# Zero-padded operands in index scores and linear attention, and a new product order in a recurrence

## The chip, the cores and the metric

One core of a Trainium2 chip runs the whole kernel. The metric is device time in microseconds, the median of several runs. The kernel before takes 2926.25 us (three runs, 2922.95 to 2929.03).

## What is computed

Two layers of a streaming encoder, 256 positions, width 2048, in float32. Each layer normalises its input, projects it with one wide matrix to the columns of four mixers, and merges the mixers' outputs behind sigmoid gates. The change touches three of the mixers:

```
# B, sparse attention: scores of all keys for each query, 8 index heads of width 64
rel   = relu(einsum('bqhd,bsd->bqhs', iq, ik))
score = einsum('bqh,bqhs->bqs', iw, rel)            # top 64 of them are kept

# A, gated linear attention, chunks of 64 positions, 4 heads (dk 128, dv 256)
k_dec = k_c * exp(total - cum)
state = state * exp(total) + einsum('bchk,bchv->bhkv', k_dec, v_c)
out   = einsum('bchk,bhkv->bchv', q_c, state)

# C, RWKV-7: a delta-rule state of 64 x 64 per head, 16 heads, here in chunks of 64
state = state*w + (state @ -kk) (kk*a)^T + v k^T ;   y = state @ r
```

D is a gated MLP that the change leaves alone. Index keys `ik` are shared by the eight heads.

## The kernel before

The 256 positions lie as two row tiles of 128 partitions. All large products go through one weight stream: SyncE fetches a block of weights of 128 x 4 x 512 (`raw`, three buffers), ScalarE rounds each 128 x 512 tile to float32r (`wh`, line 154 by `act`), VectorE takes the rest (`wl`, line 157 by `tt`), three buffers each, and TensorE adds three products for each operand pair: high x high, high x low, low x high (`mm` where positions are the output's rows, `mc` and `mb` where channels are too). All matrix products are recorded at line 169, transposes at 173, whatever calls them, so rows are told apart by tile names.

The order on each engine is set by a scheduler, which places instructions by priority and by its own simulated times; each engine then runs its list in order. Stream products thus stand between the small products of a mixer and fill TensorE while those wait for ScalarE or VectorE.

The three places that the change touches:

* **Index scores** (`b_index`). For each row tile `t` and index head one product `psc` of the head's 64 channels (`iqT`, on partitions 0 to 63 or 64 to 127 by the head's parity) with the keys `ikT`, which lie twice, once on either half of the partitions (made in `small`). ScalarE takes the ReLU into `rl`, VectorE adds it with weight `iw` into `bias`, and then finds the top 64 with eight rounds of MAX and MATCH_REPLACE in the same tile. On the same VectorE list stand the 62 steps of a triangular solve (`slv`, `slvt`) of the recurrence.
* **Recurrence** (`c_chain`). For each chunk `q` and each half `g` of the heads: `pW` (for q > 0 a 128 x 128 product of `AR` and state `sbd`, and for each of two heads a product of `G` with `VU` on 64 output rows), copied to `wbd`; `pU` from `wbd`, copied to `VU`; `pS` for the next state; `pY` for the output. All four live in a PSUM ring of two buffers (`pc`).
* **Linear attention** (`a_head`). For each head and row tile two products `pkv` of 64 positions each (keys with decay times values, one chunk each), VectorE chains them into states `aS`, and two products `pao` of 64 query positions each with the chunk's state fill the halves of one output tile.

A ring `zz` of two tiles of 128 x 1024, filled with zeros by GpSimd (`zero_padded`, line 492), holds operands whose other half stays zero: `arbd`, `wbd`, `sbd`.

Of the kernel before, what the change touches and what calls it, by code (L numbers as in the profile page):

```python
# [16 lines left out]
I32 = mybir.dt.int32  # L17
AF = mybir.ActivationFunctionType
OP = mybir.AluOpType
# [109 lines left out]
class Trunk:  # L129
# [188 lines left out]
    def rope_tables(self):  # L318
        nc = self.nc
        inv = self.inv  # L320
        pi = self.one([128, 2], "posi", I32)
        nc.scalar.dma_start(pi, self.i["positions"].rearrange("b (t p) -> p (b t)", p=128))
        pf = self.one([128, 2], "posf")
        nc.vector.tensor_copy(pf, pi)
        tb = lambda name: self.one([128, 2, 16], name)
        ang, n1, n2, tmp = tb("ang"), tb("n1"), tb("n2"), tb("rtmp")
        for t in range(2):
            self.ts(ang[:, t, :], inv, pf[:, t:t + 1], OP.mult)
        magic = 12582912.0
        i2 = float(np.float32(1.0 / (2.0 * np.pi)))  # L330

        def rnd(o, a, f):
            self.ts(o, a, f, OP.mult, magic, OP.add)
            self.ts(o, o, -magic, OP.add)


        rnd(n1, ang, i2 / 4096.0)
        self.stt(tmp, n1, -4096.0 * 2.0 * np.pi, ang, OP.mult, OP.add)
        rnd(n2, tmp, i2)
        for c in TWO_PI:  # L340
            self.stt(ang, n1, -4096.0 * c, ang, OP.mult, OP.add)
            self.stt(ang, n2, -c, ang, OP.mult, OP.add)
        rnd(n2, ang, i2)
        for c in TWO_PI:
            self.stt(ang, n2, -c, ang, OP.mult, OP.add)
        lim = 3.1415925
        self.ts(ang, ang, lim, OP.min, -lim, OP.max)
        self.sin, self.cos = tb("sin"), tb("cos")
        self.act(self.sin, ang, AF.Sin)
        self.ts(tmp, ang, -1.0, OP.mult)  # L350
        self.tt(tmp, tmp, ang, OP.max)
        self.ts(tmp, tmp, -1.0, OP.mult, float(np.float32(np.pi / 2)), OP.add)
        self.act(self.cos, tmp, AF.Sin)
        self.dump("cos", self.cos)
        self.dump("sin", self.sin)
# [86 lines left out]
    def small(self):  # L442
        nc, l = self.nc, self.l
        pa = self.product(self.xT, KT, 280, range(9), range(9))
        s = self.t("ev", [128, 2, 280], "small")
        for t in range(2):
            self.act(s[:, t, :], pa[t])
        self.w2 = self.t("s8", [97, 2, 1024], "w2")
        for a, b in ((0, 96), (96, 97)):
            nc.scalar.dma_start(self.w2[a:b], self.i["w2"][l, a:b])  # L450

        ps = self.pm([128, 2, 256], "trS")
        for j in range(2):
            for t in range(2):
                self.tr(ps[0:96, j, t * 128:(t + 1) * 128], s[:, t, j * 96:(j + 1) * 96])
        c = self.t("t2", [96, 2, 257], "lrc")
        nc.gpsimd.memset(c[:, :, 0:1], 0.0)
        self.act(c[:, :, 1:257], ps[0:96])
        d = self.t("t2", [96, 2, 256], "lrd")
        self.tt(d, c[:, :, 0:256], c[:, :, 1:257], OP.subtract)  # L460
        wT, aT = self.one([97, 256], "wT"), self.one([97, 256], "aT")
        nc.gpsimd.memset(wT, 1.0)
        nc.gpsimd.memset(aT, 1.0)
        self.stt(wT[0:96], d[:, 0, :], self.pcol[0:96, 48:49], c[:, 0, 1:257], OP.mult, OP.add)
        self.act(wT[0:96], wT[0:96], AF.Tanh)
        self.stt(aT[0:96], d[:, 1, :], self.pcol[0:96, 49:50], c[:, 1, 1:257], OP.mult, OP.add)
        self.wT, self.aT = wT, aT

        pg = self.pm([128, 256], "pg")
        for t in range(2):  # L470
            self.tr(pg[0:16, t * 128:(t + 1) * 128], s[:, t, 192:208])
        self.gT = self.one([17, 256], "gT")
        nc.gpsimd.memset(self.gT, 1.0)
        self.act(self.gT[0:16], pg[0:16])

        ik = s[:, :, 208:272].rearrange("p t (h d) -> p t h d", h=1)
        self.rope(ik, 8, 1, 2)
        ikd = self.t("s1", [128, 2, 2, 64], "ikd")
        nc.vector.tensor_copy(ikd, s[:, :, 208:272].unsqueeze(2).to_broadcast([128, 2, 2, 64]))
        pk = self.pm([128, 256], "pk")  # L480
        for t in range(2):
            self.tr(pk[:, t * 128:(t + 1) * 128], ikd[:, t].rearrange("p a d -> p (a d)"))
        self.ikT = self.one([128, 256], "ikT")
        self.act(self.ikT, pk)
        self.iw = self.one([128, 2, 8], "iw")
        self.ts(self.iw, s[:, :, 272:280], 512.0 ** -0.5, OP.mult)

# [176 lines left out]
    def c_chain(self, ys):  # L664

        nc = self.nc
        H = [slice(0, 64), slice(64, 128)]
# [3 lines left out]
        wbd, sbd = self.zero_padded("wbd"), self.zero_padded("sbd")  # L671
        for q in range(4):
            t, par = q // 2, q % 2
# [2 lines left out]
            G = self.t("s8", [128, 8, 2, 128], "Gq")  # L676
            nc.scalar.dma_start(G, self.Gd[:, qi])

            for g in range(2):
                pw = self.pc([128, 4, 128], "pW")  # L680
                for p in range(4):
                    if q:
                        self.mm(pw[:, p, :], self.AR[g][:, p, q].rearrange("p a t -> p (a t)"),
                                sbd[:, g][:, p].rearrange("p h v -> p (h v)"), p == 0, False, skip_group_check=True)
                    for h in range(2):
                        self.mm(pw[0:64, p, H[h]], G[:, 4 * g + p, 0, H[h]], self.VU[g][:, p, q, H[h]],
                                q == 0 and p == 0 and h == 0, True, skip_group_check=True)
                for h in range(2):
                    nc.vector.tensor_copy(wbd[:, g][H[h], :, h, :], pw[0:64, :, H[h]])
                if q:  # L690
                    self.act(Ys[g][O, t], pw[64:128])
# [7 lines left out]
            if q < 3:  # L699
                for g in range(2):  # L700
# [4 lines left out]
                    for h in range(2):  # L705
                        o = sbd[:, g][H[h], :, h, :]
# [56 lines left out]
    def b_index(self):  # L763
        nc = self.nc
# [5 lines left out]
        iqT = self.t("ev", [128, 4, 256], "iqT")  # L770
        for j in range(0, 4, 2):
            ps = self.pm([128, 2, 256], "piq")
# [5 lines left out]
        sc = self.bias  # L778
        for t in range(2):
            nk = 128 * (t + 1)  # L780
            for h in range(8):
                s = slice((h % 2) * 64, (h % 2) * 64 + 64)
                ps = self.pm([128, nk], "psc")
                self.mm(ps, iqT[s, h // 2, t * 128:(t + 1) * 128], self.ikT[s, 0:nk])
                rl = self.t("s1", [128, nk], "rl")
                self.act(rl, ps, AF.Relu)
                w = self.iw[:, t, h:h + 1]
                if h == 0:
                    self.ts(sc[:, t, 0:nk], rl, w, OP.mult)
                else:  # L790
                    self.stt(sc[:, t, 0:nk], rl, w, sc[:, t, 0:nk], OP.mult, OP.add)
            nc.vector.memset(sc[0:64, t, nk - 64:nk], NEG)
            if t == 1:
                self.dump("score", sc[:, 1, :])
            for _ in range(8):
                m8 = self.one([128, 8], "m8", bufs=2)
                nc.vector.max(m8, sc[:, t, 0:nk])
                nc.vector.match_replace(sc[:, t, 0:nk], m8, sc[:, t, 0:nk], HIT)
            self.ts(sc[:, t, 0:nk], sc[:, t, 0:nk], THR, OP.is_ge, BIG, OP.mult)
# [58 lines left out]
    def a_decay(self):  # L858
        nc = self.nc
# [15 lines left out]
        for t in range(2):  # L875
# [3 lines left out]
                self.mm(pt[:, h, 2 * t:2 * t + 2], lg[:, t, h * 128:(h + 1) * 128], self.ind)  # L879
            self.act(ex[:, t, :], pz, AF.Exp, scale=1.0 / 16)  # L880
        self.aex = ex
        self.atot = self.one([128, 4, 4], "atot")
        self.act(self.atot, pt, AF.Exp, scale=1.0 / 16)
        self.hg = self.t("bs", [128, 256], "hg")
# [2 lines left out]
    def a_head(self, h, g, ys):  # L887
        nc = self.nc
        pa = self.product(self.xT, KT, 512)
        m = self.t("ev", [128, 2, 512], "qkv")  # L890
        for t in range(2):
            self.act(m[:, t, :], pa[t])
        self.tt(m[:, :, 128:256], m[:, :, 128:256], self.aex[:, :, h * 128:(h + 1) * 128], OP.mult)
        ps = self.pm([128, 256], "paq")
        for t in range(2):
            self.tr(ps[:, t * 128:(t + 1) * 128], m[:, t, 0:128])
        qT = self.t("s1", [128, 256], "aqT")
        self.act(qT, ps, scale=128.0 ** -0.5)
        y = self.t("t2", [128, 2, 256], "ay")
        ss = self.one([128, 2], "ass", bufs=2)  # L900
        S = None
        for t in range(2):
            H = [slice(0, 64), slice(64, 128)]
            pk = [self.pc([128, 256], "pkv") for _ in range(2)]
            for par in range(2):
                self.mm(pk[par], m[H[par], t, 128:256], m[H[par], t, 256:512])
            Sq = []
            for par in range(2):
                q = 2 * t + par
# [6 lines left out]
                Sq.append(Sn)  # L916
            po = self.pm([128, 256], "pao")
            for par in range(2):
                q = 2 * t + par
                self.mm(po[H[par]], qT[:, q * 64:(q + 1) * 64], Sq[par])  # L920
            self.act(y[:, t, :], po, AF.Square, accum_out=ss[:, t:t + 1])
            self.rsqrt(ss[:, t:t + 1], ss[:, t:t + 1], 1.0 / 256, EPS)
            self.stt(y[:, t, :], po, ss[:, t:t + 1], self.hg, OP.mult, OP.mult)
# [149 lines left out]
```

## Time and profile before

| what | value |
|---|---|
| median of three runs | 2926.25 us |
| profiled execution | 2923.81 us, of it span 2922.0 us |
| mean granted TensorE clock | 0.997 |
| TensorE busy | 2878.9 us, 99% |
| VectorE busy | 1860.6 us, 64% |
| ScalarE busy | 1470.6 us, 50% |
| GpSimd busy | 196.6 us, 7% |
| DMA | 183 GB/s, 48.1% of the engines' time on the weight queue |

Busy time of TensorE counts pipelined products whose ends are modelled, so what a product costs is read from the starts of the products around it. A product with plain f32 operands shows as two records. `128*64` in a row means 128 rows and 64 columns of the array, `64*128` the reverse.

### The profile page before, as it was taken

Reading aid. Unit: us, or ns where it says so; the run is one execution under the profiler, and the core shown is the slowest. Engines: PE = TensorE matmul, PEld = TensorE weight load, DVE = VectorE, ACT = ScalarE, POOL = GpSimd, SP = SyncE. Lnnn points to the kernel's source line nnn. Section 1 sums busy time; section 2 is a strip of 40 time slices with the busy share of each in tenths; the row PEclk is TensorE's granted clock in tenths of the full one; section 3 lists DMA queues with packets and bytes.
Section 4 is the critical chain, followed back from the end, with each engine's and each line's share of the span. In section 5 each row is a group of like instructions: output and inputs, shape, how many; then the busy total and the mean of one; then the engine's idle time right before and its main releaser. Section 6 shows DMA issues by size and latency. Waiting matters only on the chain.

```text
span 2922.0 us, 44230 instructions
## 1 busy us (share of the span) xinstructions
PE 2878.9 (99%) x16880; PEld 2465.0 (84%) x16880; DVE 1860.6 (64%) x3347; ACT 1470.6 (50%) x2632; POOL 196.6 (7%) x291
## 2 busy tenths in 40 slices
PE   7999999999999999999989999999999999999998
PEld 6998888887778898888789988888877788988886
DVE  6787857655555655556568878575555556565565
ACT  6554544545444545445565555345554444454454
POOL 1222001000000000000022220110000000000000
PEclk9999999999999999999999999999999999999999
DMA  5555545555445565555555565355554555555554
GB/s 184 186 192 184 181 149 176 181 187 185 163 166 193 188 213 191 187 190 186 181 178 188 188 206 167 136 185 186 188 180 161 176 189 202 195 192 190 190 185 158
DMA packets 100796, 533.51 MB, mean 183 GB/s; under 512 B 30852, under 2 KB 31108, under 8 KB 40742
## 3 DMA queue, kind: packets, MB, share of 16 engines
q1 hardware_dynamic: 68256, 486.96, 48.1%
q10 hardware_dynamic: 26568, 24.85, 2.8%
q0 software_dynamic: 5760, 18.88, 2.0%
q8 instruction: 132, 2.16, 0.3%
q14 instruction: 80, 0.66, 0.1%
HBM read 512.83 MB, written 17.83 MB: 182 GB/s over the span
## 4 chain that ended last, share of the span: by engine, by line
PE 79%; issue 16%; DVE 2%; ACT 1%; DMA 1%; ACTq 0%; POOL 0%; DVEq 0%; POOLq 0%
PE mm L169 48%; PE mc L169 15%; PE mb L169 6%; PE pW L169 1%; DVE wl L157 1%; ACT wh L154 1%; PE pG L169 1%; PE pao L169 1%; PE pY L169 1%; PE pU L169 1%; PE pkv L169 1%; PE trT L173 0%; PE psc L169 0%; PE plg L169 0%; PE po L169 0%
## 5 line engine op out<-in xcount | busy, mean ns | idle before, releaser
L157 DVE TENSOR_TENSOR wl<-raw,wh 128x512 fp32r<-128x512 f32 (+1 forms) x1822 | 1255.0, 693 | 885.0 <-ACT wh L154 879.5
L154 ACT ACTIVATE wh<-raw 128x512 fp32r<-128x512 f32 (+1 forms) x1822 | 1145.8, 630 | 1264.8 <-DVE wl L157 619.4
L169 PE MATMUL mm<-wh,xT 128*128 128x512 f32 (+1 forms) x4216 | 1332.0, 393 | 2.6 <-ACT wh L154 2.6
L169 PEld LDWEIGHTS mm<-wh,xT 128*128 128x128 f32 x4216 | 784.3, 188 | 179.0 <-issue 7.9
L169 PE MATMUL mm<-wl,xT 128*128 128x512 f32 (+1 forms) x2108 | 829.5, 394 | 0.6 <-DVE wl L157 0.6
L169 PE MATMUL mc<-xT,wh 128*128 128x256 f32 x3072 | 529.1, 282 | 0.0
L169 PEld LDWEIGHTS mm<-wl,xT 128*128 128x128 f32 x2108 | 396.0, 188 | 94.6 <-DVE wl L157 9.9
L169 PEld LDWEIGHTS mc<-xT,wh 128*128 128x128 f32 x3072 | 448.5, 189 | 2.1
L169 PE MATMUL mc<-xT,wl 128*128 128x256 f32 x1536 | 385.1, 286 | 0.2
L169 PE MATMUL mm<-wh,yT 128*128 128x512 f32 x1024 | 321.1, 389 | 0.0
L169 PEld LDWEIGHTS mc<-xT,wl 128*128 128x128 f32 x1536 | 266.2, 189 | 2.1 <-DVE wl L157 0.8
L169 PEld LDWEIGHTS mm<-wh,yT 128*128 128x128 f32 x1024 | 192.1, 188 | 41.5 <-ACT aex L154 1.5
L169 PE MATMUL mm<-wl,yT 128*128 128x512 f32 x512 | 199.4, 389 | 0.0
L169 PE MATMUL mb<-wh,xT 128*128 128x256 f32 x512 | 118.5, 284 | 0.0
L169 PEld LDWEIGHTS mm<-wl,yT 128*128 128x128 f32 x512 | 96.1, 188 | 19.9
L169 PE MATMUL mb<-xT,wh 128*128 128x256 f32 x512 | 103.1, 283 | 0.0
L169 PEld LDWEIGHTS mb<-wh,xT 128*128 128x128 f32 x512 | 87.6, 188 | 1.8 <-issue 1.0
L169 PEld LDWEIGHTS mb<-xT,wh 128*128 128x128 f32 x512 | 79.1, 188 | 2.4 <-issue 2.0
L169 PE MATMUL mb<-wl,xT 128*128 128x256 f32 x256 | 74.0, 289 | 0.0
L169 PE MATMUL mb<-xT,wl 128*128 128x256 f32 x256 | 72.8, 284 | 0.0
L183 POOL TENSOR_TENSOR orsq<-orsq,mhalf 128x1 f32<-128x1 f32 x4 | 2.3, 587 | 887.1 <-DVE orsq L163 887.0
L169 PE MATMUL mm<-wown,xT 128*128 128x280 f32 (+1 forms) x204 | 49.4, 389 | 8.1 <-ACT xT L154 5.3
(278 smaller groups left out, 2027.1 us busy)
## 6 DMA issues: line engine op xcount, KB each, us to landing
raw<-in_w_dram SPq DMA_DIRECT2D x456, 1024.0 KB, 4.8
Gd<-G POOLq DMA_DIRECT2D x32, 256.0 KB, 3.5
Gq<-Gd ACTq DMA_DIRECT2D x8, 1024.0 KB, 5.1
raw<-in_w_dram SPq DMA_DIRECT2D x8, 560.0 KB, 3.9
bsd<-bs POOLq DMA_DIRECT2D x16, 256.0 KB, 5.1
bs<-bsd POOLq DMA_DIRECT2D x16, 256.0 KB, 3.7
x<-in_x_dram ACTq DMA_DIRECT2D x4, 512.0 KB, 6.1
x<-in_x_dram SPq DMA_DIRECT2D x4, 512.0 KB, 7.0
```

Source lines behind the costliest of these rows:

```text
L154: self.nc.scalar.activation(out, in_, f, **kw)
L157: (eng or self.nc.vector).tensor_tensor(out, a, b, op)
L169: self.nc.tensor.matmul(out, lhsT, rhs, start=start, stop=stop, **kw)
L183: self.nc.gpsimd.tensor_tensor(out, out, self.mhalf[:, :n], OP.pow)
```

## The change

Keys `ikT` become two tiles of 128 partitions, each with one half zero; one product of all 128 channels gives two heads' scores side by side, so four products of twice the columns stand for eight. `kz` and `qz`, two zero-padded buffers each for even and odd heads, hold the decayed keys and the scaled queries of linear attention; `pkv` contracts over 128 positions of which 64 are zero, and the two `pao` of a row tile add into all 128 output rows. In the recurrence both `pW` tiles are allocated first, all full products of both halves `g` are called first, and then those of half width. The rope tables' scratch moves from tiles of its own to ring slots; `rl` moves from ring `s1` to `t2`.

```diff
-        self.ikT = self.one([128, 256], "ikT")
-        self.act(self.ikT, pk)
+        self.ikT = self.one([128, 2, 256], "ikT")
+        nc.gpsimd.memset(self.ikT, 0.0)
+        for a in range(2):
+            self.act(self.ikT[a * 64:a * 64 + 64, a, :], pk[a * 64:a * 64 + 64])
...
+            pws = [self.pc([128, 4, 128], "pW") for _ in range(2)]
+            if q:
+                for g in range(2):
+                    for p in range(4):
+                        self.mm(pws[g][:, p, :], self.AR[g][:, p, q].rearrange("p a t -> p (a t)"),
+                                sbd[:, g][:, p].rearrange("p h v -> p (h v)"), p == 0, False, skip_group_check=True)
             for g in range(2):
-                pw = self.pc([128, 4, 128], "pW")
+                pw = pws[g]
                 for p in range(4):
-                    if q:
-                        self.mm(pw[:, p, :], self.AR[g][:, p, q].rearrange("p a t -> p (a t)"),
-                                sbd[:, g][:, p].rearrange("p h v -> p (h v)"), p == 0, False, skip_group_check=True)
                     for h in range(2):
                         self.mm(pw[0:64, p, H[h]], G[:, 4 * g + p, 0, H[h]], self.VU[g][:, p, q, H[h]],
...
-            for h in range(8):
-                s = slice((h % 2) * 64, (h % 2) * 64 + 64)
-                ps = self.pm([128, nk], "psc")
-                self.mm(ps, iqT[s, h // 2, t * 128:(t + 1) * 128], self.ikT[s, 0:nk])
-                rl = self.t("s1", [128, nk], "rl")
+            for j in range(4):
+                ps = self.pm([128, 2, nk], "psc")
+                self.mm(ps, iqT[:, j, t * 128:(t + 1) * 128], self.ikT[:, :, 0:nk])
+                rl = self.t("t2", [128, 2, nk], "rl")
                 self.act(rl, ps, AF.Relu)
...
+        self.kz, self.qz = (self.zero_padded(n).rearrange("p b q a t -> p (b q a t)").rearrange(
+            "p (b t a k) -> p b t a k", b=2, t=2, a=2) for n in ("akz", "aqz"))
...
-        self.tt(m[:, :, 128:256], m[:, :, 128:256], self.aex[:, :, h * 128:(h + 1) * 128], OP.mult)
+        kz, qz = self.kz[:, h % 2], self.qz[:, h % 2]
+        for a in range(2):
+            self.tt(kz[H[a], :, a, :], m[H[a], :, 128:256], self.aex[H[a], :, h * 128:(h + 1) * 128], OP.mult)
...
-        qT = self.t("s1", [128, 256], "aqT")
-        self.act(qT, ps, scale=128.0 ** -0.5)
+        for t in range(2):
+            o = qz[:, t]
+            self.act(bass.AP(tensor=o.tensor, offset=o.offset, ap=[o.ap[0], [192, 2], [1, 64]]),
+                     ps[:, t * 128:(t + 1) * 128].rearrange("p (a t) -> p a t", a=2), scale=128.0 ** -0.5)
...
-                self.mm(pk[par], m[H[par], t, 128:256], m[H[par], t, 256:512])
+                self.mm(pk[par], kz[:, t, par], m[:, t, 256:512])
...
-                q = 2 * t + par
-                self.mm(po[H[par]], qT[:, q * 64:(q + 1) * 64], Sq[par])
+                self.mm(po, qz[:, t, par], Sq[par], par == 0, par == 1)
```

TensorE, the recurrence, chunk q = 1 of layer 0, before (`AR` rows are the full products, `VU,Gq` those of half width):

```order
L169 MATMUL mm_5364<-wh,xT 128x512
L169 MATMUL mm_5365<-wh,xT 128x512
L169 MATMUL mm_5365<-wl,xT 128x512
L169 MATMUL pW<-sbd,AR 128x128
L169 MATMUL pW<-VU,Gq 64x64 x2
L169 MATMUL pW<-sbd,AR 128x128
L169 MATMUL pW<-VU,Gq 64x64 x2
```

The same place of the changed kernel, with what follows:

```order
L169 MATMUL mm_5335<-wl,xT 128x512
L169 MATMUL pW<-sbd,AR 128x128 x8
L169 MATMUL pW<-VU,Gq 64x64 x16
L173 MATMUL ppt<-cst,lg 128x128 x4
L169 MATMUL po<-PT,bv 128x128 x2
L169 MATMUL mm_5335<-wh,xT 128x512
```

Eight alternations have become one run of full products and one of half width. In chunk q = 2 the scheduler splits them into four full, two half, four full and fourteen half, in q = 3 into four, eight, four and eight with stream products between.

TensorE, linear attention, head 0 of layer 0, before:

```order
L169 MATMUL mm_7879<-wh,xT 128x512
L169 MATMUL pkv<-qkv 128x256 x2
L169 MATMUL mm_7878<-wh,xT 128x512
L169 MATMUL mm_7879<-wh,xT 128x512
L169 MATMUL mm_7878<-wl,xT 128x512
```

and after:

```order
L169 MATMUL mm_7854<-wh,xT 128x512
L169 MATMUL pkv<-qkv,akz 128x256
L169 MATMUL mm_7853<-wh,xT 128x512
L169 MATMUL mm_7854<-wh,xT 128x512
L169 MATMUL pkv<-qkv,akz 128x256
L169 MATMUL mm_7853<-wl,xT 128x512
```

The two first `pkv` of a head stood together and now have two stream products between them; the later `pkv` and `pao` stand as before, one `pao` ahead of a `pkv` twice and two `pao` alone.

VectorE, the score stage of layer 0, where the first row tile's scores end (the MEMSET on `bias` ends them; `m_` are the top-k's maxima), before:

```order
L166 SCALAR_TENSOR_TENSOR bias<-rl,iw,bias 128x128
L157 TENSOR_TENSOR wl<-raw,wh 128x512
L161 TENSOR_SCALAR bias<-rl,iw 128x256
L157 TENSOR_TENSOR slv<-slv,slvt 128x11x21
L792 MEMSET bias 64x64
L166 SCALAR_TENSOR_TENSOR bias<-rl,iw,bias 128x256
L157 TENSOR_TENSOR slvt<-slv 128x12x20
L797 MAX m_4244<-bias 128x8
L157 TENSOR_TENSOR wl<-raw,wh 128x512
```

and after:

```order
L166 SCALAR_TENSOR_TENSOR bias<-rl,iw,bias 128x128
L157 TENSOR_TENSOR slv<-slv,slvt 128x8x24
L157 TENSOR_TENSOR wl<-raw,wh 128x512
L796 MEMSET bias 64x64
L157 TENSOR_TENSOR slvt<-slv 128x9x23
L801 MAX m_4230<-bias 128x8
L161 TENSOR_SCALAR bias<-rl,iw 128x256
L157 TENSOR_TENSOR slv<-slv,slvt 128x9x23
L802 MATCH_REPLACE bias<-m_4230,bias 128x128
L166 SCALAR_TENSOR_TENSOR bias<-rl,iw,bias 128x256
```

The first row tile's scores end three steps of the solve earlier, and its top-k begins with fewer weight splits ahead of it.

## Rows read from the trace of the kernel before

**Rows 1.** The page's first part: busy us (share of the span) x instructions by engine.
```profile
PE 2878.9 (99%) x16880; PEld 2465.0 (84%) x16880; DVE 1860.6 (64%) x3347; ACT 1470.6 (50%) x2632; POOL 196.6 (7%) x291
```

**Rows 2.** What TensorE waited for: us in total, times, longest us.
```profile
PE trT L173 <- DVE x L161: 11.5, 1, 11.5
PE trT L173 <- DVE o L161: 9.1, 1, 9.1
...
PE psc L169 <- ACT iqT L154: 1.6, 1, 1.6
```

**Rows 3.** The chain that ended last, two merged pieces: start us, us, what.
```profile
56.28 16.97 PE mc L169 x144
...
557.95 110.91 PE mm L169 x486
```

**Rows 4.** TensorE's timeline, a plain f32 product: start us, us, engine, line, what, count.
```profile
681.54 0.40 PE L169 MATMUL mm<-wh,xT 128*128 128x512 f32 x1
681.77 1.02 PE L169 MATMUL paz<-alog,cst 128*128 128x512 f32 x2
682.23 0.80 PE L169 MATMUL mm<-wh,xT 128*128 128x512 f32 x1
682.86 0.39 PE L169 MATMUL mm<-wl,xT 128*128 128x512 f32 x1
```

**Rows 5.** TensorE's timeline, a pair of score products, and a single one.
```profile
303.05 0.85 PE L169 MATMUL mm<-wh,xT 128*128 128x512 f32 x3
303.83 0.49 PE L169 MATMUL psc<-ikT,iqT 64*128 64x128 f32 x4
304.26 0.50 PE L169 MATMUL mm<-wl,xT 128*128 128x512 f32 x1
304.60 0.39 PE L169 MATMUL mm<-wh,xT 128*128 128x512 f32 x1
...
316.59 0.28 PE L169 MATMUL mb<-wh,xT 128*128 128x256 f32 x1
316.80 0.70 PE L169 MATMUL psc<-ikT,iqT 64*128 64x256 f32 x2
317.42 0.38 PE L169 MATMUL mb<-xT,wl 128*128 128x256 f32 x1
317.64 0.28 PE L169 MATMUL mb<-xT,wh 128*128 128x256 f32 x1
```

**Rows 6.** TensorE's timeline, one round of the recurrence's pW.
```profile
413.09 0.45 PE L169 MATMUL pW<-VU,Gq 128*64 128x64 f32 x4
413.47 0.49 PE L169 MATMUL pW<-sbd,AR 128*128 128x128 f32 x2
413.89 0.45 PE L169 MATMUL pW<-VU,Gq 128*64 128x64 f32 x4
```

**Rows 7.** Stretches: length; PE, PEld, DVE, ACT, POOL busy (x); PEclk, DMA share, GB/s.
```profile
729.34:742.37 13.03, 13.03 (x51) 7.64 (x50) 6.72 (x14) 4.43 (x9) 0.58 (x1) 1.00 0.42 158
300.00:345.00 45.00, 45.00 (x291) 37.90 (x291) 42.46 (x131) 25.16 (x54) 0.00 (x0) 1.00 0.46 164
1750.00:1795.00 45.00, 45.00 (x291) 37.92 (x291) 42.23 (x129) 24.63 (x52) 0.00 (x0) 1.00 0.47 159
480.00:510.00 30.00, 30.00 (x187) 26.69 (x186) 28.49 (x64) 18.73 (x40) 8.49 (x10) 1.00 0.62 215
1930.00:1960.00 30.00, 30.00 (x187) 26.74 (x186) 28.49 (x63) 18.86 (x40) 8.51 (x10) 1.00 0.66 215
```

**Rows 8.** Timelines of VectorE and of TensorE: one weight split and its first product.
```profile
342.65 0.67 DVE L157 TENSOR_TENSOR wl<-raw,wh 128x512 fp32r<-128x512 f32 x1
...
343.56 0.39 PE L169 MATMUL mm<-wl,xT 128*128 128x512 f32 x1
```

**Rows 9.** Timelines of VectorE and GpSimd: the decayed keys, and a zero fill.
```profile
726.72 0.42 DVE L157 TENSOR_TENSOR qkv<-qkv,aex 128x256 f32<-128x256 f32 x1
...
470.79 0.96 POOL L492 MEMSET wbd<- 128x1024 f32 x1 [4.82 <-PE pU L169]
```

More of the change, by code (lines that the diff above doesn't have):

```diff
@@ L320, in rope_tables @@
         inv = self.inv
-        pi = self.one([128, 2], "posi", I32)
+        pi = self.t("c1", [128, 2], "posi", I32)
         nc.scalar.dma_start(pi, self.i["positions"].rearrange("b (t p) -> p (b t)", p=128))
-        pf = self.one([128, 2], "posf")
+        pf = self.t("c1", [128, 2], "posf")
         nc.vector.tensor_copy(pf, pi)
-        tb = lambda name: self.one([128, 2, 16], name)
-        ang, n1, n2, tmp = tb("ang"), tb("n1"), tb("n2"), tb("rtmp")
+        ang, n1, n2, tmp = (self.t("s1", [128, 2, 16], n) for n in ("ang", "n1", "n2", "rtmp"))
         for t in range(2):
@@ L347, in rope_tables @@
         self.ts(ang, ang, lim, OP.min, -lim, OP.max)
-        self.sin, self.cos = tb("sin"), tb("cos")
+        self.sin, self.cos = (self.one([128, 2, 16], n) for n in ("sin", "cos"))
         self.act(self.sin, ang, AF.Sin)
@@ L780, in b_index @@
             nk = 128 * (t + 1)
-            for h in range(8):
-                s = slice((h % 2) * 64, (h % 2) * 64 + 64)
-                ps = self.pm([128, nk], "psc")
-                self.mm(ps, iqT[s, h // 2, t * 128:(t + 1) * 128], self.ikT[s, 0:nk])
-                rl = self.t("s1", [128, nk], "rl")
-                self.act(rl, ps, AF.Relu)
[L787 to L791, printed above, removed]
+            for j in range(4):
+                ps = self.pm([128, 2, nk], "psc")
+                self.mm(ps, iqT[:, j, t * 128:(t + 1) * 128], self.ikT[:, :, 0:nk])
+                rl = self.t("t2", [128, 2, nk], "rl")
+                self.act(rl, ps, AF.Relu)
+                for a in range(2):
+                    w = self.iw[:, t, 2 * j + a:2 * j + a + 1]
+                    if j + a == 0:
+                        self.ts(sc[:, t, 0:nk], rl[:, a], w, OP.mult)
+                    else:
+                        self.stt(sc[:, t, 0:nk], rl[:, a], w, sc[:, t, 0:nk], OP.mult, OP.add)
             nc.vector.memset(sc[0:64, t, nk - 64:nk], NEG)
@@ L892, in a_head @@
             self.act(m[:, t, :], pa[t])
-        self.tt(m[:, :, 128:256], m[:, :, 128:256], self.aex[:, :, h * 128:(h + 1) * 128], OP.mult)
+        H = [slice(0, 64), slice(64, 128)]
+        kz, qz = self.kz[:, h % 2], self.qz[:, h % 2]
+        for a in range(2):
+            self.tt(kz[H[a], :, a, :], m[H[a], :, 128:256], self.aex[H[a], :, h * 128:(h + 1) * 128], OP.mult)
         ps = self.pm([128, 256], "paq")
@@ L902, in a_head @@
         for t in range(2):
-            H = [slice(0, 64), slice(64, 128)]
             pk = [self.pc([128, 256], "pkv") for _ in range(2)]
             for par in range(2):
-                self.mm(pk[par], m[H[par], t, 128:256], m[H[par], t, 256:512])
+                self.mm(pk[par], kz[:, t, par], m[:, t, 256:512])
             Sq = []
```

## The prediction

> **What bounds the kernel now.** I read the page's busy line first, then who TensorE waited for, then the chain, and only then TensorE's timeline in the three places that the change touches. TensorE is busy for 2878.9 of 2922.0 us [rows 1]. The longest of its waits stand at the two layer starts, where nothing else can run [rows 2]; it does not wait at the edited places except once, 1.6 us, for the first score. The chain is one run of TensorE after another: 486 products of 512 columns in 110.91 us, 0.228 us each, and 144 of 256 columns in 16.97 us, 0.118 us each [rows 3]. So the question is how much TensorE time the edited products take out of this stream, and whether the engines that feed it can follow.
>
> **What an f32 product costs.** The stream's operands are float32r; the edited products are plain f32, and each shows as two records. I price a block by the start of a stream product behind it minus the start of one ahead of it, less 0.228 or 0.118 us for each stream product between. A full-array f32 product of 512 columns: 682.86 - 681.54 - 2 x 0.228 = 0.86 us [rows 4]. I take half of it, 0.43, for 256 columns and a quarter, 0.22, for 128.
>
> **Scores.** Two products of 64 rows and 128 columns, on the two row halves, start together and cost 304.60 - 303.05 - 4 x 0.228 = 0.64 us as a block; a single one of 256 columns costs 317.64 - 316.59 - 2 x 0.118 = 0.81 [rows 5]. A layer has five blocks of the first width (three of them pairs, two singles at the same price, since the second product of a pair runs beside the first) and seven of the second (one pair): 5 x 0.64 + 7 x 0.81 = 8.9 us. After it there are four full products of 256 columns and four of 512: 4 x 0.43 + 4 x 0.86 = 5.2. TensorE gains 3.7 us a layer. What goes is not arithmetic: the 0.64 holds 0.22 of streaming and about 0.4 of standing still on entering and leaving the half array.
>
> **Recurrence.** One round of a full product and two half-width ones takes 413.89 - 413.09 = 0.80 us [rows 6]. The full one is 0.22; a half-width one has 64 columns and takes a little over an eighth of 0.86, 0.12, two of them 0.24. The remaining 0.34 us is the change from full array to half width and back. There are eight such rounds in each of three chunks, 24 a layer. In the new order one chunk has one change there and back and two have two, because the scheduler still splits them (four full, two half, four full, fourteen half in one of them): 5 instead of 24, 19 x 0.34 = 6.5 us a layer. The neighbouring half-width products (pU, pS, pY) lie closer together too, six changes there and back fewer over both layers, 6 x 0.34 / 2 = 1.0. Together 7.5 us a layer.
>
> **Linear attention.** From 729.34 to 742.37, one head's products and what stands between them: 13.03 us with 50 weight loads, 16 of them for the head's eight f32 products, so 34 x 0.228 = 7.75 of stream and 5.3 us for the head [rows 7]. After it eight full products of 256 columns: 8 x 0.43 = 3.5. Gain 1.8 a head, 7.0 a layer.
>
> So TensorE gains 3.7 + 7.5 + 7.0 = 18.2 us a layer, 36.4 us in all, if nothing else holds it.
>
> **What holds it.** In linear attention VectorE is busy for 6.72 of 13.03 us [rows 7]: all of the 7.0 shows. In the score stretch VectorE is the tight engine: 42.46 of 45 us in layer 0, 42.23 in layer 1 [rows 7], since the top-k and the triangular solve share it with the weight splits. At 343.56 TensorE takes a wl that VectorE finished at 342.65 + 0.67 = 343.32 [rows 8], 0.24 us ahead. TensorE can come there earlier only by what VectorE has left: 2.54 us idle plus 0.24, less what the new order puts ahead of that split. By the order and this trace's durations that is some 0.8 us more, since score sums and top-k steps now run earlier. That leaves at most 2.0, and not all small gaps close; I take 1.2 of the 3.7 a layer (ends: 0 and 3.7, the latter if the stretch can lend slack from behind).
> The recurrence's own stretch has VectorE half free, but its norms and outputs come about five weight tiles later in the new order, into a stretch like 480 to 510 us, where VectorE is busy for 28.49 of 30 us in both layers [rows 7]. I take off 0.9 a layer of 7.5 (ends: 0, and half of the gain).
> Sum: (1.2 + 6.6 + 7.0) x 2 = 29.6 us.
>
> **Edits at nothing.** Each head has one VectorE instruction and one ScalarE instruction more: the k product becomes two of half the partitions, each at most the 0.42 us of the one at 726.72 [rows 9]. That one ends at 727.14, the first pkv starts at 729.67, so 2.5 us cover it; if that cover were gone, 0.4 us a head, 3 us in all. The two zero fills in a_decay take about 0.96 us each on GpSimd, as the one of wbd does [rows 9]; they stand 200 us ahead of their use. In layer 0 they take the place of two fills for the next layer that wait for the same readers; in layer 1 they are added between the norm's powers, 1.9 us on an engine with nothing tight behind it. The next layer's fills now wait for the last head, hundreds of us before they are wanted. ScalarE has four score activations a row tile instead of eight. The rope tables use ring slots that are free at the start: nothing. A wait that is added: pU needs a buffer of the ring of which pW now holds both; it had to wait for the first pW's copies anyway.
>
> The profiled run took 2923.81 us, so 2894.2 for one like it; the median of the runs is 2.4 above it: **2896.6 us**.
>
> **Rivals.** First, everything shows: VectorE's order adapts and the score stretch gives 3.7 too. 2926.3 - 36.4 = 2890. For it: the solve's steps have slack after 360 us. Against: the 0.24 us.
> Second, VectorE takes more: nothing from the scores, half of the recurrence, (0 + 3.8 + 7.0) x 2 = 21.6: 2905. For it: at some ten splits of the score stretch the new order has 2 to 6 us more VectorE work ahead than the old.
> Third, the zero padding doesn't do its work: the standing still in scores and linear attention comes with each entry of f32 into the float32r stream, not with the half arrays. Then a head keeps six entries (8 x 0.43 + 6 x 0.34 = 5.5 us where 5.3 stood), the scores eight (5.2 + 8 x 0.4 = 8.4 of 8.9), and only the recurrence gains: 0.8 lost and 0.5 gained beside 6.6, 6.3 a layer, 2914. Against: the 512-column product enters and leaves with no such gap [rows 4].
> Fourth, slower: the half arrays earn more than they cost. Wherever VectorE sets the stream's pace, a removed gap returns as a wait, while the pairs are lost. Pairs that ran at once are, a layer, three of 128 columns (0.22 each), one of 256 (0.43) and four in linear attention (0.43 each): 2.8 us, 5.6 in all, with 0.8 x 2 of VectorE work ahead: 2933. It decides only where VectorE has no slack left in all three places; rows 7 show that in one.
> The Trainium skill's page "TensorEngine Tiling (Array Packing)" (Overview, Theoretical Speedup) speaks for this fourth one: a contraction of 64 may run up to twice as fast as two row tiles, so padding it to 128 gives that away. The pair in rows 5 agrees that two products take the time of one, and by the rule alone the sum would be those 5.6 us of loss. What it leaves out here is the standing still around each block.
>
> **How the numbers follow.** Forecast 0.54, its own range 2892 to 2902; all shows 0.21; VectorE takes more 0.17; padding without effect 0.02; slower 0.03. The other 0.03 I leave for a wait that I have not seen and that eats the gain to within 0.2%, 5.9 us, about what a measurement of this kernel can tell from no change. The range of eight in ten goes from 2888 (the first rival, with 2 us for its terms) to 2907 (the second, likewise). Faster by over 0.2% holds the first four cases, 0.94; within 0.2% 0.03; slower 0.03.
>
> **What would show it.** Right: in linear attention pkv and pao cost 0.43 each and the stream product behind them starts without delay; one pW block of eight full records pairs and sixteen half-width ones near 4.0 us where 6.4 stood; score products at 0.43 and 0.86; and TensorE then waiting for wl between 300 and 345 us, about 2.5 us a layer. Wrong: no such waits (first rival); waits for wl, wbd or VU of over 3 us a layer behind the recurrence (second); gaps of 0.3 us around pkv and pao as before (third). A time above 2907 would mean that a removed gap comes back as a wait in linear attention or in the recurrence too.

## The result, and the profile after

The changed kernel takes 2894.05 us (median of four runs, 2893.21 to 2894.72) beside 2924.76 us for the kernel before on the same chip: a ratio of 0.9893, interval 0.9876 to 0.9910. The forecast was 2896.6, or 29.6 us less in the profiled run; the profiled spans are 2922.0 and 2892.3 us, 29.7 less. The sum came out almost exactly, but by luck: two deductions in it met nothing, and an edit that it put at nothing cost about as much as they took off.

Busy time of the engines, the page's first part:

```profile
PE 2849.4 (99%) x16848; PEld 2487.1 (86%) x16848; DVE 1859.9 (64%) x3355; ACT 1467.8 (51%) x2626; POOL 202.1 (7%) x297
```

TensorE has 29.5 us less than in [rows 1]; the others stand where they were. What it waited for (us in total, times, longest):

```profile
PE trT L173 <- DVE x L161: 11.5, 1, 11.5
PE trT L173 <- DVE o L161: 9.4, 1, 9.4
...
PE psc L169 <- ACT iqT L154: 1.8, 2, 1.3
PE mm L169 <- DVE wl L157: 0.6, 2, 0.3
...
PE mb L169 <- DVE wl L157: 0.3, 1, 0.3
```

Against [rows 2] nothing new: waits for a weight split `wl` come to 0.9 us in the whole run, where I had forecast about 2.5 a layer in the score stretch alone.

The edited products, in TensorE's timeline (start us, us, engine, line, what, count). Linear attention:

```profile
724.14 0.59 PE L169 MATMUL pkv<-qkv,akz 128*128 128x256 f32 x2
724.38 0.58 PE L169 MATMUL mm<-wl,xT 128*128 128x512 f32 x1
724.80 0.40 PE L169 MATMUL mm<-wh,xT 128*128 128x512 f32 x1
```

This `pkv` costs 724.80 - 724.14 - 0.227 = 0.43 us. All eight of a head, priced in this way, come to 3.51 where I had 3.5. The recurrence's block that answers to the rounds of [rows 6]:

```profile
416.03 1.95 PE L169 MATMUL pW<-sbd,AR 128*128 128x128 f32 x16
417.90 2.08 PE L169 MATMUL pW<-VU,Gq 128*64 128x64 f32 x32
419.91 0.66 PE L173 MATMUL ppt<-cst,lg 128*128 128x128 f32 x4
```

419.91 - 416.03 = 3.88 us where eight rounds of 0.80 stood (4.0 forecast). And a score product, beside [rows 5]:

```profile
310.99 0.84 PE L169 MATMUL mm<-wh,xT 128*128 128x512 f32 x3
311.67 1.02 PE L169 MATMUL psc<-ikT,iqT 128*128 128x512 f32 x2
312.12 0.80 PE L169 MATMUL mm<-wl,xT 128*128 128x512 f32 x1
312.76 0.40 PE L169 MATMUL mm<-wh,xT 128*128 128x512 f32 x1
```

312.76 - 310.99 - 4 x 0.227 = 0.86. So the edited blocks cost what I had said, within 0.1 us. But the 0.227 in these lines was 0.228 before, and that is where the unexpected part begins. The same two pieces of the chain as in [rows 3] (start us, us, what):

```profile
56.74 17.27 PE mc L169 x144
...
552.82 110.17 PE mm L169 x486
```

144 untouched products of 256 columns take 17.27 us where they took 16.97, and 486 of 512 columns 110.17 where they took 110.91. The stream itself has changed its pace, in both directions.

To see what that is worth I went through all starts of TensorE's products in both traces and put each interval down to the stream's kind or to the small block between (one block being priced as above). Us won over both layers:

| part | full price in the prediction | forecast | measured |
|---|---|---|---|
| scores | 7.4 | 2.4 | 6.5 |
| recurrence | 15.0 | 13.2 | 15.4 |
| linear attention | 14.0 | 14.0 | 13.5 |
| stream, 512 columns (mm of x) | 0 | 0 | 11.4 |
| stream, 256 columns (mc and mb) | 0 | 0 | -17.7 |
| the rest | 0 | 0 | 0.6 |
| sum | 36.4 | 29.6 | 29.7 |

### The profile page after: what moved, and what is told of

Read it like the earlier page. It is cut to its first block, busy times and chain, and to the rows that moved or that the text cites. A ratio compares the mean times of both kernels' runs of the same rounds, so it can differ in the third digit from the quotient of the medians.

```text
span 2892.3 us, 44157 instructions
## 1 busy us (share of the span) xinstructions
PE 2849.4 (99%) x16848; PEld 2487.1 (86%) x16848; DVE 1859.9 (64%) x3355; ACT 1467.8 (51%) x2626; POOL 202.1 (7%) x297
## 4 chain that ended last, share of the span: by engine, by line
PE 94%; DVE 2%; ACT 1%; DMA 1%; issue 1%; ACTq 1%; POOL 0%; DVEq 0%; POOLq 0%
PE mm L169 60%; PE mc L169 19%; PE mb L169 7%; DVE wl L157 1%; PE pW L169 1%; PE pG L169 1%; ACT wh L154 1%; PE trT L173 1%; PE pU L169 1%; PE pY L169 1%; PE pao L169 0%; PE pkv L169 0%; PE po L169 0%; PE psc L169 0%; DMA Gd<-G 0%
## 5 line engine op out<-in xcount | busy, mean ns | idle before, releaser
L169 PE MATMUL mc<-xT,wh 128*128 128x256 f32 x3072 | 540.5, 285 | 0.0
L169 PEld LDWEIGHTS mc<-xT,wh 128*128 128x128 f32 x3072 | 457.2, 192 | 2.1
```

Of the source, the lines that this page charges most:

```text
L169: self.nc.tensor.matmul(out, lhsT, rhs, start=start, stop=stop, **kw)
```

## Experiments

Each version of the kernel stands beside the kernel before on the same chip. Three chips were used (the kernel before took 2924.27, 2923.51 and 2924.47 us), so times from different chips are best compared by these ratios.

**The pace of the stream by itself.** The change moves the rope tables' scratch into the rings `c1` and `s1`, which are now allocated ahead of the weights, and so shifts what lies behind them. By the kernels' allocation x (`xT`) starts at byte 53792 of a partition in both; the first weight tile `wh` starts at 161120 before and at 167712 after. That distance is 64 bytes modulo 256 before, 0 after (832 and 256 modulo 1024). A kernel without the layers runs TensorE's two kinds of products at 28 pairs of such starts (27 different ones, four of them with x 64 bytes further):

```
for xs, ws in QUIET:        # bytes: start of x, start of weights
    36 x mm(pm[t], X[xs + ...128 cols], W[ws + ...512 cols])   # "m": weights move
    72 x mm(pc[j], W[ws + ...128 cols], X[xs + ...256 cols])   # "c": x moves
for xs, ws in BUSY:         # the same beside 26 splits on ScalarE and VectorE
```

> A test of TensorE alone, the two layers left out: 36 products of 512 columns (x stationary) and 72 of 256 columns (weights stationary, x moving) for each of 28 distances in bytes between the weights' and x's start in a partition, and again for five of them with ScalarE and VectorE splitting tiles beside it. In the changed kernel the weights lie 448 bytes further from x than before (distance 256 modulo 1024 where it was 832), products of 512 columns with x start 0.227 us apart where they stood at 0.229 to 0.232, and those of 256 columns 0.120 where they stood at 0.118 and 0.113. Theory placement: the distance alone sets this, so at 832 the test shows 0.229 to 0.232 and 0.118, at 256 it shows 0.227 and 0.120, in the quiet part already. Rival contention: the pace comes from ScalarE and VectorE or the DMA writing beside TensorE, so the quiet part shows one pace at all distances. Rival issue: it comes from how the instructions are fetched, so no distance shows it.

TensorE's timeline; `q0w64m` is weights moved at x 0, weights 64, `b` the part with busy engines:

```profile
76.77 8.42 PE L36 MATMUL q0w64m<-W,X 128*128 128x512 f32 x36
85.03 8.34 PE L36 MATMUL q0w64c<-X,W 128*128 128x256 f32 x72
93.20 8.57 PE L36 MATMUL q0w96m<-W,X 128*128 128x512 f32 x36
...
177.83 8.37 PE L36 MATMUL q0w256m<-W,X 128*128 128x512 f32 x36
186.04 8.79 PE L36 MATMUL q0w256c<-X,W 128*128 128x256 f32 x72
194.67 8.56 PE L36 MATMUL q0w288m<-W,X 128*128 128x512 f32 x36
...
362.94 8.56 PE L36 MATMUL q0w832m<-W,X 128*128 128x512 f32 x36
371.34 8.35 PE L36 MATMUL q0w832c<-X,W 128*128 128x256 f32 x72
379.52 8.53 PE L36 MATMUL q0w896m<-W,X 128*128 128x512 f32 x36
...
480.54 8.35 PE L36 MATMUL b0w0m<-W,X 128*128 128x512 f32 x36
488.73 8.79 PE L36 MATMUL b0w0c<-X,W 128*128 128x256 f32 x72
497.36 8.56 PE L36 MATMUL b0w64m<-W,X 128*128 128x512 f32 x36
505.76 8.35 PE L36 MATMUL b0w64c<-X,W 128*128 128x256 f32 x72
```

From start to start, at distance 64: (85.03 - 76.77) / 36 = 0.229 us with weights moved and (93.20 - 85.03) / 72 = 0.1135 with x moved. At 256: 0.228 and 0.120. At 832: 0.233 and 0.1136. With the other engines busy: 0.2275 and 0.120 at 0, and (505.76 - 497.36) / 36 = 0.233 with weights moved at 64. So TensorE alone shows that the place matters, and in the main it goes by the distance modulo 256. At 0 the wide products are quickest (0.227 to 0.228), and those that move x are at 0.120. At 64 those that move x are quickest (0.1135), and the wide ones take 0.229 or 0.233. All other distances lie between 0.232 and 0.234 and between 0.117 and 0.120, and the pairs with x 64 bytes further fall in with their distance. Contention and issue fall as causes of this order.

Two things do not fit theory placement. At 832 it expected 0.229 to 0.232 and 0.118, and the test shows 0.233 and 0.1136. And one pair of starts, at the distance 64, gave 0.229 quiet and 0.233 busy. So the distance does not settle the pace at 64 by itself.

The Trainium skill's page "SBUF — State Buffer" (Terms, and Who interferes with whom) says that TensorE reads through ports of its own and never waits for another engine. Wide products at the other four busy distances agree with their quiet ones within 0.001 us; at 64 they differ by 0.004, and no run here shows whether the other engines cause that.

**The place alone in the kernel before.**

```diff
         tb = lambda name: self.one([128, 2, 16], name)
+        self.one([128, 112], "pad")
```

> The kernel before with one unused tile of 448 bytes a partition ahead of the weights: every engine's list of instructions stays word for word, only the weights, and what is allocated behind them, lie where the changed kernel has them relative to x. Theory placement: products of 512 columns with x go from about 0.230 to 0.227 us (12 us saved over both layers), those of 256 columns from 0.118 to 0.120 (18 us lost): 2924.8 + 6 = about 2931 us. Rival: the pace belongs to the new order or to what runs beside it, not to the place: 2924.8 within 2 us, and the rows stay at 0.229 to 0.232 and 0.118.

Measured 2928.3 us beside 2924.27: ratio 1.0013, interval 1.0005 to 1.0022. The two pieces of the chain now read as in the changed kernel:

```profile
56.86 17.27 PE mc L169 x144
562.80 110.21 PE mm L169 x486
```

An unused tile of 448 bytes costs 4 us, with a few us of play (the interval is 1.5 to 6.4), and in the profiled run 4.4 (spans 2922.0 and 2926.4). The 6 expected are inside. Since the rows moved with the place and not with the order, the rival falls.

**The recurrence alone** (the hunk of `c_chain` on the kernel before).

> The kernel before with the recurrence's new product order alone; the weights stay in their old place. Theory full: every term of TensorE shows, the recurrence gives 7.7 us a layer as its blocks in the changed kernel's trace say: 2924.8 - 15.4 = 2909.4. Theory of the prediction: 0.9 a layer is given back in the stretch behind it where VectorE is full: 2924.8 - 13.2 = 2911.6. Rival of half: 2917.

Measured 2911.43 beside 2924.27: 0.9959, 0.9944 to 0.9975. The interval holds both of the first theories and ends where the third begins (2917). The trace has the blocks 14.4 us cheaper and the span 14.1 shorter (2907.9 for 2922.0), so all but 0.3 showed in that run.

**Linear attention alone** (the hunks of `a_decay` and `a_head` on the kernel before).

> The kernel before with the zero-padded operands of linear attention alone; the weights stay in their old place. Blocks of the changed kernel's trace say 6.7 us a layer: 2924.8 - 13.4 = 2911.4. The prediction's 7.0 a layer: 2910.8. Rival (padding without effect, the standing still comes with each entry of f32 into the stream): 2925 or slower. Rival (pairs lost, gaps return as waits): 4 x 0.43 x 2 = 3.4 slower, 2928.

Measured 2909.63: 0.9952, 0.9939 to 0.9966, 14.6 us. Its blocks give 6.85 a layer where 7.0 was forecast. Both rivals fall: the half array does carry a cost of its own, and the pairs lost weigh less. The profiled run is the longest of its four, which lie between 2908.2 and 2914.9, and in it the wide stream products took 3.5 us more. Its granted clock says why (columns as in [rows 7]):

```profile
300.44:303.85 3.41, 3.41 (x10) 2.61 (x10) 2.92 (x11) 1.72 (x5) 0.00 (x0) 0.50 0.98 384
```

The clock stood at 0.50, the lower of its two levels (1.2 GHz), in this stretch, and again from 1740.86 to 1744.28. TensorE had waited for 1.5 us shortly before the first (for `iqT`) and for 1.6 before the second (for `wh`). The two stretches last 6.8 us together, and at half the clock 3.4 of these are lost. In the kernel before the clock stays at 1.00 behind the same wait of 1.6 us for `iqT`; in the run of the recurrence alone it fell once, from 300.11 to 303.52.

**Where in x the products start.** The test showed 0.1135 at the distance of the kernel before, where that kernel mostly had 0.118.

> TensorE alone again, the layers left out, with products of 256 columns behind a stationary x as a third kind, and x starting 32 bytes off a multiple of 64 as it does in both kernels. In the first test a distance of 64 modulo 256 between weights and x gave 0.1135 us for products that move x and 0.229 to 0.233 for those that move weights; 0 modulo 256 gave 0.120 and 0.227. Theory start: the kernel before, also at 64 modulo 256, showed 0.118 where this gave 0.1135, because x and weights both start 32 bytes off; so with x at 32 the test shows 0.118 at the distance 64, and 0.1135 only with x at 0. Rival: the kernel's 0.118 comes from the other engines and the DMA, and the test shows 0.1135 with x at 32 as well.

`q32w96` has x 32 bytes off and the distance 64:

```profile
138.50 8.41 PE L35 MATMUL q32w96m<-W,X 128*128 128x512 f32 x36
146.75 8.35 PE L35 MATMUL q32w96c<-X,W 128*128 128x256 f32 x72
154.94 4.43 PE L35 MATMUL q32w160h<-W,X 128*128 128x256 f32 x36
...
176.12 4.26 PE L35 MATMUL q32w224h<-W,X 128*128 128x256 f32 x36
180.22 8.56 PE L35 MATMUL q32w224m<-W,X 128*128 128x512 f32 x36
```

(154.94 - 146.75) / 72 = 0.114. The 32 bytes do nothing here: that theory falls for TensorE alone. Wide products read 0.229 at 832 in this test, where the first test had 0.233.

The third kind (`h`, 256 columns with the weights moved) reads 0.120 at 0, 0.118 at 64 and (180.22 - 176.12) / 36 = 0.114 at 192, that is with x 64 bytes beyond the weights modulo 256. For both kinds of 256 columns, then, the quick place is where the stationary operand starts 64 bytes beyond the moving one.

**The old distance in the changed kernel.**

```diff
+        self.iw = self.one([128, 2, 8], "iw")
         pa = self.product(self.xT, KT, 280, range(9), range(9))
...
-        self.iw = self.one([128, 2, 8], "iw")
```

> The changed kernel with one small tile (iw) allocated ahead of the weights instead of behind them: the lists of instructions stay word for word, the weights lie 64 bytes further from x, at 320 where 256 stood (64 modulo 256, as in the kernel before). Theory placement by distance modulo 256: products that move weights rise from 0.227 to about 0.229 to 0.232 (12 us lost), those that move x fall from 0.120 to 0.118 or 0.113 (18 us won): 2894 - 6 = 2888. Rival (only the kernel's old place modulo 1024 does it): 2894, rows as in the changed kernel.

Measured 2891.87 beside 2923.51: 0.9891, 0.9878 to 0.9905, a profiled span of 2890.7 for 2892.3.

```profile
56.59 16.97 PE mc L169 x144
547.89 110.92 PE mm L169 x486
```

The rows come back to those of [rows 3], so 64 bytes do it and the old place is not needed. It is the rows that decide here: the span is 1.6 us shorter where 6 were expected, and the interval is nearly that of the changed kernel (0.9876 to 0.9910). Put down to the kinds, mc and mb win 13 to 14 us and wide products of x lose 11 to 12; small waits take some of the rest (for wl 2.3 us in all, 0.9 in the changed kernel).

**Each kind at its better distance.**

```diff
-                    wh = self.one([128, width], "wh", F32R, bufs=SPLIT_BUFS)
-                    wl = self.one([128, width], "wl", F32R, bufs=SPLIT_BUFS)
+                    wh, wl = (self.at(self.one([128, 576], z, F32R, bufs=SPLIT_BUFS), width, place) for z in ("wh", "wl"))
...
+        o = 16 if place == "mc" else 0
+        return z[:, o:o + width]
...
+        self.one([128, 8], "pad")
```

> The changed kernel with x starting on a multiple of 64 bytes, and weights at distance 0 modulo 256 where they are moved and 64 modulo 256 where x is moved (each split tile has 64 bytes more, SP moves to ring s1 to make room). Theory placement: 0.227 stays for 512 columns, products that move x (4608 of mc and half of the 1536 of mb) go from 0.120 to 0.1135: 5376 x 0.0063 = 34 us: 2894 - 34 = 2860. Rival (the engines that feed the stream set the pace of these stages as soon as TensorE gets faster): TensorE waits for wh, wl or raw there, and less than half shows, 2877 or more.

Measured 2874.84 beside 2923.51: 0.9833, 0.9818 to 0.9848; 19.5 us of span less than the changed kernel, more than the rival allows and less than the theory.

```profile
56.17 16.34 PE mc L169 x144
546.71 110.17 PE mm L169 x486
...
2451.56 58.50 PE mc L169 x516
```

In these stretches mc stands at 0.1134, with wide products at 0.227. Waits for wl come to 3.4 us, 2.5 more than in the changed kernel, a small part of the 15 that are missing. The rest is in mc and mb themselves: of 4486 intervals between two mc products some two thirds are at 0.113 and 0.114, most others at 0.117 and 0.118, and mb won next to nothing. The half of mb that moves weights was put at the distance 0, where the test above has 0.120 for its kind.

**x off by 32 bytes in this version** (the pad of 8 becomes 16).

> The last version with x and the weights both 32 bytes further, so that x starts 32 bytes off a multiple of 64 again; distances stay 0 and 64 modulo 256, the lists of instructions word for word. In that version products that move x stood at 0.113 and 0.114 for 65 of 100 and at 0.117 and 0.118 for most others; in the kernel before, and in the changed one with its weights at 320, at the same distance, mostly at 0.118. Theory start (x 32 bytes off costs 0.004 us a product, though the test of TensorE alone did not show it): 0.118 becomes the rule again, 2874.8 + about 9 = 2884. Rival (the spacing of the split tiles, 2304 bytes where it was 2048, or chance of the phase brings the 0.113): 2875, rows as in the last version.

Measured 2877.12 beside 2924.47: 0.9835, 0.9821 to 0.9848, 2.8 us of span more, on another chip.

```profile
56.54 16.96 PE mc L169 x144
...
2454.46 58.52 PE mc L169 x516
```

Neither theory: one stretch is back at 0.1178, another stays at 0.1134, in one kernel at one distance. At 64 modulo 256 there are two paces (in the test too: 0.229 and 0.233 for wide products), and which of them a stretch gets stays open.

**Scores alone** (the hunks of `rope_tables`, `small` and `b_index` on the kernel before), with the weights in the changed kernel's place.

> The changed kernel with linear attention and the recurrence's order as before: padded index scores alone, weights in the changed kernel's place, so the baseline is the kernel before with its weights moved there, 2928.3. Theory full (the trace of the changed kernel shows no waits for wl worth naming between 300 and 345 us): 3.2 us a layer, 2921.9. Theory of the prediction (VectorE lends only 1.2 a layer): 2925.9, with TensorE waiting for wl in the score stretch about 2 us a layer. Rival (nothing shows): 2928.3.

Measured 2922.5 beside 2923.51: 0.9994, 0.9985 to 1.0003, that is 0.0019 under the kernel before with moved weights, 5.5 us; the spans differ by 5.3 (2926.4 and 2921.1). Forecast by the prediction 2.4, by the full price 6.4. The difference of two ratios is known to some 3.6 us either way, so the time rules out a gain of nothing but hardly tells 2.4 from 6.4. The waits do: for wl they come to 0.9 us in this run, where the prediction's theory wanted about 2 a layer. So the score gain shows nearly whole.

**A test of the 0.34 us.** pU was left half-width by the change.

```diff
-                    self.mm(pu[U, p, :], self.TT[:, qi * 8 + 4 * g + p, :], ...)
+                    j = qi * 8 + 4 * g + p
+                    full, b = (j > 0, j - 1) if par == 0 else (j < 31, j)
+                    if full:
+                        self.mm(pu[:, p, :], self.TT[:, b:b + 2, :]..., ...)
```

> The version of 2874.8 us, and pU's half-width products made full: the 128 columns of TT hold a second head's block, whose rows of the result nobody reads; only the first or last block, where TT ends, stays half. A pU block of four half-width products costs 1.21 us, full ones 4 x 0.22 = 0.87, since entering and leaving the half array goes. Theory (the change of array shape costs 0.34 us there and back, whatever stands in it): six of eight blocks a layer, 2 x 6 x 0.34 = 4.1 us: 2870.7. Rival (the standing still comes with plain f32 products in the stream, full or half): 2874.8.

Measured 2871.01 beside 2924.47: 0.9817, 0.9804 to 0.9831; 4.0 us of span less than the version of 2874.8, which ran on another chip and whose interval overlaps this one. The scheduler also moved other products, so the block itself is the direct reading. One block of four products, half-width and then full:

```profile
441.77 0.28 PE L169 MATMUL mb<-xT,wh 128*128 128x256 f32 x1
441.99 1.09 PE L169 MATMUL pU<-wbd,TT 128*64 128x128 f32 x8
443.00 0.39 PE L169 MATMUL mb<-xT,wh 128*128 128x256 f32 x1
443.23 0.28 PE L169 MATMUL mb<-xT,wl 128*128 128x256 f32 x1
```

```profile
441.31 0.28 PE L169 MATMUL mb<-xT,wh 128*128 128x256 f32 x1
441.43 1.05 PE L169 MATMUL pU<-wbd,TT 128*128 128x128 f32 x8
442.24 0.36 PE L169 MATMUL mb<-xT,wh 128*128 128x256 f32 x1
442.44 0.28 PE L169 MATMUL mb<-xT,wl 128*128 128x256 f32 x1
```

Less 2 x 0.118 of stream: 443.23 - 441.77 - 0.236 = 1.22, and 442.44 - 441.31 - 0.236 = 0.89. The same four products without a change of shape are 0.33 cheaper. It is the change that costs, and not each half-width product: in the pW block above sixteen of them in a row take 419.91 - 417.90 = 2.01 us, 0.126 each, near the 0.12 that I had taken for one. The Trainium skill's page "TensorEngine Tiling (Array Packing)" (Key Properties) says that changing the tiling mode drains TensorE; this is what it costs here, there and back. This is also the quickest version: 53 us under the kernel before, about 23 under the changed one.

## Why the prediction was right, and where it was not

*The prices.* f32 products of 0.22, 0.43 and 0.86 us and 0.34 for a change of shape held in the blocks shown: 35.4 us measured for the three parts, 36.4 at full price. Of the rivals the third (padding without effect) and the fourth (pairs) are refuted by the blocks and by the runs of single parts. The second (VectorE takes more) falls with the waits that it needs: for wl they are 0.9 us in the whole run.

*What VectorE holds, 1.2 of 3.7 a layer.* This step failed: 3.2 a layer shows. I counted VectorE's idle time from 300 us, 2.5 us, and bounded the gain by it. Here is the run of 26 splits that ends with the one of [rows 8], in the kernel before and in the changed one (columns as in [rows 7]):

```profile
295.10:343.32 48.22, 46.64 (x296) 38.65 (x295) 41.90 (x127) 26.19 (x55) 0.00 (x0) 1.00 0.51 172
```

```profile
299.97:344.84 44.87, 43.54 (x280) 38.07 (x279) 41.32 (x131) 24.08 (x43) 0.53 (x1) 1.00 0.54 185
```

VectorE was idle for 48.22 - 41.90 = 6.3 us before, and for 3.6 after. Most of the idle time stood just ahead of my window, and the new order used it: VectorE's work is about the same, and it does the same 26 splits in 3.4 us less. The split itself is still only just in time, but no later than before:

```profile
344.17 0.67 DVE L157 TENSOR_TENSOR wl<-raw,wh 128x512 fp32r<-128x512 f32 x1
...
345.20 0.39 PE L169 MATMUL mm<-wl,xT 128*128 128x512 f32 x1
```

345.20 - 344.84 = 0.36 us ahead, where it was 0.24.

*What is given back behind the recurrence, 0.9 a layer.* Not seen. VectorE is as full there as I had said:

```profile
480.00:510.00 30.00, 30.00 (x170) 25.81 (x170) 28.59 (x65) 18.71 (x40) 8.09 (x10) 1.00 0.60 209
```

Yet TensorE is busy for all of the 30 us. The time of the recurrence alone could not have decided this.

*Rope scratch in ring slots, "nothing".* This step failed too, and not by the instructions, which cost nothing: it moved all weights by 448 bytes modulo 1024. That is worth -17.7 and +11.4, some 6 us lost, and by the run with the pad alone about 4. My two deductions, 6.8 us, stood for engines that did not hold anything; the loss that took their place was of the same size by chance. In mechanism the first rival (everything shows, 2890) was nearer than my forecast, and by the sign that I had set for it, no waits for wl, it was the one whose condition held; the pace of the stream stands between its 2890 and the 2894 measured.

## What to carry to other kernels

A small f32 product between stream products costs its columns (here 0.22 us for 128) plus a price for each change of array shape (here 0.34 there and back between full array and half width), so count the changes in the order of TensorE's list before counting arithmetic. When an engine is to cap a gain, measure its idle time from the last point where it stood ahead, not from where the edit begins. And when tiles are added or moved, look where the large operands land: compare the pace of products that nobody touched.

## What the hardware showed that I had not expected

The pace of a float32r product depends on the distance between its operands' starts in a partition, in the main modulo 256 bytes. With 512 moving columns of weights: 0.227 to 0.228 us at 0, 0.229 or 0.233 at 64, 0.232 to 0.234 elsewhere. With 256 moving columns of x (twelve products to a tile): 0.120 at 0, 0.1135 or 0.118 at 64, 0.117 to 0.120 elsewhere. With 256 moving columns of weights 0.114 is found at 192. Over the 4608 mc products of this kernel the better distance was worth about 19 us against the changed kernel, more than any single part of the change; some 13 of these the change itself had lost. Why there are two paces at 64 is open.
